# Inverting the 16x16 diagonal blocks of the RWKV-7 chunks row by row on GpSimd instead of by doubling levels on VectorE

## The chip, the cores and the metric

The kernel runs on one core of one Trainium2 chip. The metric is the device time of one execution in microseconds (us). A core has a matrix engine (TensorE, PE in the profile), three engines for elementwise work (VectorE = DVE, ScalarE = ACT, GpSimd = POOL) and a queue that issues DMAs (SyncE = SP). Each engine takes its instructions strictly in the order in which the program lists them; between engines only semaphores order the work.

## The reference, cut to what matters

One block of a hybrid encoder on 256 tokens of width 2048: a norm, one input projection shared by a Mamba-2 SSD mixer and an RWKV-7 time mixer, one output projection, a SwiGLU feed-forward part and a last norm, all in float32. The change is in the RWKV-7 mixer, whose recurrence is, for each of 32 heads of width 64:

```
def step(S, inp):
    r_t, w_t, k_t, v_t, a_t, b_t = inp
    sa = jnp.einsum('bhvk,bhk->bhv', S, a_t)
    S = S * w_t[:, :, None, :] + sa[..., None] * b_t[:, :, None, :] + v_t[..., None] * k_t[:, :, None, :]
    return S, jnp.einsum('bhvk,bhk->bhv', S, r_t)
```

The kernel evaluates it in four chunks of 64 tokens. Inside a chunk the terms `sa` depend on each other through a strictly lower triangular 64x64 matrix N, so the kernel needs the inverse of (I - N) for each head and chunk. It builds that inverse from the inverses X of the 16x16 diagonal blocks, then joins them to 32x32 and 64x64 with small matmuls on TensorE.

## The kernel before, in words

Every large matmul is written as three float32r matmuls: weights arrive by DMA as `raw` tiles (four buffers, SP queue), ScalarE copies them to `whi` (line 192), VectorE subtracts to get `wlo` (line 193), and TensorE multiplies both parts (lines 277 to 279 with 256 columns, 305 to 307 with 512). There are four buffers each of `whi` and `wlo`.

RWKV-7 heads are processed in eight pairs of 128-channel blocks (four heads, times four chunks = 16 head-chunks, times four diagonal blocks = 64 blocks of 16x16). While TensorE runs the projection for one pair, the mixer work of the two previous pairs is interleaved with it. `Side` is a list of functions with due times; every half tick (12 large matmuls of `gemm_a`, or six of `gemm_b`) it emits what is due. A window for a pair is 12 ticks long for the first windows and 16 or more later, when it also holds an output projection. The tables `AMATS`, `INV` and `CHAIN` at the top hold the due ticks. The tile framework then schedules: the order of each engine's queue is fixed when the program is built, by what it expects to be ready, and need not be the emitted one.

The steps for one pair that matter here, in order of dependence:

- `amat("atb", ...)` (lines 602 to 625): TensorE forms N for all chunks (`ps_a`), VectorE masks it.
- `inv_out`: VectorE picks the 16x16 diagonal blocks into `dg` (line 633), SP writes them to a scratch in DRAM (`sc_n`, line 635) and reads them back with one block per partition (`nb`, 64 partitions, line 637). GpSimd sets `xb` to the identity (lines 640 and 641).
- `inv_level(1, 2, 4, 8)`: VectorE doubles the size of the inverted blocks in `xb`: a copy (line 659), then for 2, 4 and 8 two products each, made of a broadcast multiply into `pd` (line 681) and a reduction into `tt` or `xb` (line 683): 1 + 8 + 8 + 4 = 21 instructions a pair.
- `inv_in`: SP writes `xb` to DRAM (`sc_X`, line 691) and reads it back as `cm` (line 694); VectorE masks `cm` into `X` (line 697) and transposes it to `XT` (line 702).
- `lev16a` to `lev32b`: small matmuls `ps_b` (line 708) with VectorE and ScalarE between them make `XF`.
- The chain of the pair before runs in the same window: for each chunk `step_r` (`ps_r`, line 762, reads the state `sn`), `step_w` (`ps_w`, line 776, then `ws` on VectorE, line 780), `step_s` (`ps_s`, lines 792 and 795, then `sn` on VectorE in two instructions, lines 800 and 801). Then `gnorm`, `gnorm2` and `final`, and the output projection `ps_o` with the adds into `h` (line 318).

Of the kernel before, what the change touches and what calls it, by code (L numbers as in the profile page):

```python
# [13 lines left out]
ALU = mybir.AluOpType  # L14
AX = mybir.AxisListType
# [17 lines left out]

PREP = (1.081, 1.2, 4.2, 5.2, 5.536, 6.756, 8.05, 9.2)
AMATS = (0.132, 1.4, 2.027, 2.231, 2.69, 3.323, 6.493)
INV = (4.9, 6.4, 7.9, 9.4, 9.9, 11.9, 12.9, 13.9, 15.9)
STEPS = (0.667, 2.0, 5.0)
SSD = (0.9, 2.7, 4.842, 6.642, 8.442, 8.924, 10.724, 12.524, 12.657, 16.124)
CHAIN = (0.05, 0.6, 1.4, 2.4, 3.4, 4.0, 4.9, 5.9, 6.5, 7.4, 8.4, 9.0, 9.9, 11.4, 12.9, 13.4)
# [29 lines left out]
def tile_hybrid_block(ctx: ExitStack, tc: tile.TileContext, x, norm1_g, w_in, conv_w, conv_b, dt_bias, A_log, D_skip,  # L69
                      ssd_norm_g, mu, w0, w2, a0, a2, g2, k_k, k_a, r_k, gn_w, gn_b, w_out, norm2_g, w_gate, w_up,  # L70
                      w_down, norm_f_g, out):
    nc = tc.nc
    PS = bass.MemoryType.PSUM
    x = x[0]
    out = out[0]
# [10 lines left out]
    side = Side()  # L86
# [7 lines left out]
    def bc(ap, n):  # L94
        return ap.unsqueeze(ap.ndim).broadcast_to(list(ap.shape) + [n])
# [3 lines left out]
    xv = x.rearrange("(b p) d -> p b d", p=P)  # L99
# [52 lines left out]
    for hh in range(2):  # L152
        for s in range(2):
            m = mask2[hh * 64:(hh + 1) * 64, s]
# [4 lines left out]
    for s in range(2):  # L159
        for hh in range(2):  # L160
            a = hh * 64
# [48 lines left out]
    def finish(i, b):  # L210
        r = rstd[i][:, b:b + 1]
        nc.vector.tensor_reduce(r, ssq[i][:, b], axis=AX.X, op=ALU.add)
        nc.scalar.activation(r, r, AF.Sqrt, bias=eps6, scale=1.0 / D)
        nc.vector.reciprocal(r, r)
        return r
# [228 lines left out]
    def rwkv_pair(pi, st):  # L444
        cb0 = 2 * pi

        def tl(name, shape=(P, 2, T), bufs=1, tag=None):
            return rp.tile(list(shape), F32, name=name, tag=tag or name, bufs=bufs)
# [141 lines left out]
        def amat(name, key, half):  # L590
            def f():
                if half == 0:
                    st[name] = tl(name, (P, NCH, 2, 64), 2)
                dst = st[name]
                src = ch(st[key])
                if name == "atb" and half == 1:
                    across(dst, src)
                    return
                ps = mxt("ps_a").rearrange("p (c t) -> p c t", c=4)
                for c in range(4):  # L600
                    for hh in range(2):
                        nc.tensor.matmul(hd(ps, hh)[:, c], hd(src, hh)[:, half * 4 + c],
                                         hd(st["ar"], hh)[:, half * 4 + c].rearrange("p a t -> p (a t)"),
                                         start=True, stop=True)
                nc.vector.tensor_tensor(dst[:, half * 4:half * 4 + 4].rearrange("p c a t -> p c (a t)"), ps,
                                        mask2.rearrange("p a t -> p (a t)").unsqueeze(1).broadcast_to([P, 4, P]),
                                        ALU.mult)
                if name == "atb":
                    d = dst[:, 0:4, 0]
                    nc.vector.tensor_tensor(d, d, bc(st["nn"][:, 0:4], 64), ALU.mult)  # L610
            return f
# [16 lines left out]
        def inv_out():  # L628
            tm = tl("t1", (P, NCH, 4, 16), 2)
            nc.vector.tensor_tensor(tm, st["atb"][:, :, 0].rearrange("p c (b t) -> p c b t", t=16),  # L630
                                    bc(bmask, 16).unsqueeze(1).broadcast_to([P, NCH, 4, 16]), ALU.mult)
            dg = tl("dg", (P, NCH, 16))
            nc.vector.tensor_reduce(dg, tm.rearrange("p c b t -> p c t b"), axis=AX.X, op=ALU.add)
            sc = dram.tile([NCH, P, 16], F32, name="sc_n")
            nc.sync.dma_start(out=sc.rearrange("c p t -> p c t"), in_=dg)
            nb = tl("nb", (64, 272))
            nc.sync.dma_start(out=nb[:, :256].rearrange("p (i t) -> p i t", t=16),
                              in_=sc.rearrange("c (x i) t -> (c x) i t", i=16))
            xb = tl("xb", (64, 272))
            nc.gpsimd.memset(xb, 0.0)  # L640
            nc.gpsimd.memset(xb[:, 0:256:17], 1.0)
            st["nb"], st["xb"] = nb, xb

        def inv_level(s):
            def f():
                nb, xb = st["nb"], st["xb"]
                nm = 8 // s

                def blocks(t, at, swap):

                    v = t[:, :nm * 34 * s].rearrange("p (m x) -> p m x", m=nm)[:, :, at:at + 16 * s]
                    v = v.rearrange("p m (j t) -> p m j t", t=16)[:, :, :, 0:s]
                    return v.rearrange("p m j t -> p m t j") if swap else v


                n21 = blocks(nb, s, False)
                x11 = blocks(xb, 0, True)
                if s == 1:
                    nc.vector.tensor_copy(blocks(xb, 16, False), n21)
                    return  # L660
                x22 = blocks(xb, 17 * s, False)
                x21 = blocks(xb, 16 * s, False)
                tt = tl("tt", (64, 64), 2)

                if s == 2:
                    cut = [(slice(0, nm), r) for r in range(s)]
                    shp = [64, nm, s, s]
                    tv = tt[:, :nm * s * s].rearrange("p (r m c) -> p m r c", r=s, c=s)
                else:
                    cut = [(m, slice(0, s)) for m in range(nm)]  # L670
                    shp = [64, s, s, s]
                    tv = tt[:, :nm * s * s].rearrange("p (m r c) -> p m r c", r=s, c=s)
                tj = tv.rearrange("p m j c -> p m c j")

                def product(out, a, b):

                    for m, r in cut:
                        pd = tl("pd", (64, 512), 2, tag="t1")
                        pv = pd[:, :shp[1] * s * s].rearrange("p (a c j) -> p a c j", c=s, j=s)
                        bb = b[:, m] if s == 2 else b[:, m].unsqueeze(1)  # L680
                        nc.vector.tensor_tensor(pv, a[:, m, r].unsqueeze(2).broadcast_to(shp), bb.broadcast_to(shp),
                                                ALU.mult)
                        nc.vector.tensor_reduce(out[:, m, r], pv, axis=AX.X, op=ALU.add)

                product(tv, n21.rearrange("p m j r -> p m r j"), x11)
                product(x21, x22, tj)
            return f

        def inv_in():
# [160 lines left out]
        def final():  # L850
# [3 lines left out]
            for j in range(2):  # L854
                for kk in range(2):
# [8 lines left out]
            nc.vector.tensor_tensor(yl, yo, yh.bitcast(F32), ALU.subtract)  # L864

        amats = [recept, sums, amat("atb", "bt", 0), amat("atb", "bt", 1), inv_out, amat("atk", "kt", 0),
                 amat("atk", "kt", 1)]
        inv = [inv_level(1), inv_level(2), inv_level(4), inv_level(8), inv_in, lev16a, lev16b, lev32a, lev32b]
        chain = [load2]
        for c in range(4):  # L870
            chain += [step_r(c), step_w(c), step_s(c)]
# [6 lines left out]
    def window(pi, ticks):  # L878
        if pi < 8:
            w = pairs[pi]  # L880
            w["load"]()
            for t, n in zip(PREP, ("decay", "rate", "keys", "keys2", "keysum", "btt", "vt", "ktt")):
                side.at(t, w[n])
        if 0 < pi < 9:
            w = pairs[pi - 1]
            for t, f in zip(AMATS, w["amats"]):
                side.at(t, f)
            for t, f in zip(INV, w["inv"]):
                side.at(t if ticks >= 16 else t * (ticks - 0.5) / 16, f)
        if pi > 1:  # L890
            for t, f in zip(CHAIN, pairs[pi - 2]["chain"]):
                side.at(t if ticks >= 16 else t * (ticks - 0.5) / 16, f)
# [5 lines left out]
    for pi in range(8):  # L898
        st = {}
        pairs.append(rwkv_pair(pi, st))  # L900
        window(pi, 16 if pi > 2 else 12)
        for i, (n, c) in enumerate((("k", CK), ("v", CV), ("r", CR))):
            ps = scaled(gemm_a(w_in, [(0, 256, c + pi * 256)], "ps_rkv"))
            t = pp.tile([P, 2, T], F32, name="rkv", tag="t" + n, bufs=1)
            for j in range(2):
                m = ((c - CR) // P) + 2 * pi + j
                shift(t[:, j], ps[:, j], omA[:, m:m + 1], colA[:, MU + m:MU + m + 1])
            st[n] = t
        out_rwkv(pi - 3)
        side.drain()  # L910


    window(8, 20)
    xzst = ExitStack()

# [6 lines left out]
    for i in range(4):  # L922
# [6 lines left out]
        for j in range(2):  # L929
            b = 2 * i + j  # L930
            conv(BC[:, b // 4, b % 4], ps[:, j], 16 + b)
    nc.scalar.activation(BC, BC, AF.Silu)
    out_rwkv(5)
    side.drain()
    window(9, 18)

    def ssd_group(g, xc, zs):
# [105 lines left out]
    for g in range(4):  # L1043
        xc = []
        for i in range(2):
            ps = scaled(gemm_a(w_in, [(0, 256, CXBC + g * 512 + i * 256)], "ps_xs"))
            t = xz.tile([P, 2, T], F32, name="xc", tag=f"xc{i}")
# [55 lines left out]
    for j in range(D_FF // 512):  # L1103
        c = j * 512
# [28 lines left out]
    for b in range(2):  # L1133
        s = slice(b * P, (b + 1) * P)
        for n, (hi, lo) in enumerate(ws):
# [5 lines left out]
            c = slice(n * 512, (n + 1) * 512)  # L1141
# [6 lines left out]
    for b in range(2):  # L1148
        r = finish(2, b)
        for n in (2, 3, 0, 1):  # L1150
            c = slice(n * 512, (n + 1) * 512)
            t = hg[b][n]
# [33 lines left out]
```

## Time and profile before

| what | value |
|---|---|
| median of three runs | 1677.11 us (1675.01 to 1679.0) |
| the profiled execution: its time / its span | 1676.59 us / 1674.5 us |
| mean granted TensorE clock | 0.996 |
| busy share PE, DVE, ACT, POOL | 98%, 72%, 54%, 1% |
| instructions on POOL | 57 |

The RWKV-7 stage fills about the first 600 us of the span, the SSD stage and its projections follow up to about 960 us, the feed-forward part is the rest. Busy time of PE overlaps: a 256-column matmul is listed with some 0.28 us but the next one starts 0.12 us later, so PE is only idle in the profile where no matmul at all is under way. "Idle before, releaser" tells what an engine waited for.

### The profile page before, as it was taken

Reading aid. Unit: us, or ns where it says so; the run is one execution under the profiler, and the core shown is the slowest. Engines: PE = TensorE matmul, PEld = TensorE weight load, DVE = VectorE, ACT = ScalarE, POOL = GpSimd, SP = SyncE. Lnnn points to the kernel's source line nnn. Section 1 sums busy time; section 2 is a strip of 40 time slices with the busy share of each in tenths; the row PEclk is TensorE's granted clock in tenths of the full one; section 3 lists DMA queues with packets and bytes.
Section 4 is the critical chain, followed back from the end, with each engine's and each line's share of the span. In section 5 each row is a group of like instructions: output and inputs, shape, how many; then the busy total and the mean of one; then the engine's idle time right before and its main releaser. Section 6 shows DMA issues by size and latency. Waiting matters only on the chain.

```text
span 1674.5 us, 31150 instructions
## 1 busy us (share of the span) xinstructions
PE 1641.6 (98%) x12514; PEld 1423.4 (85%) x12514; DVE 1199.3 (72%) x1907; ACT 910.5 (54%) x1488; POOL 17.7 (1%) x57
## 2 busy tenths in 40 slices
PE   8999999999999999999999999999999999999997
PEld 8988888898898998998988888888888888888886
DVE  7888889888898877978778655465465564554657
ACT  6655765757656556667565544444444444444444
POOL 3000000000000000000000000000000000000000
PEclk9999999999999999999999999999999999999999
DMA  9644545445455456675654666666666666666663
GB/s 248 180 127 111 145 125 149 133 133 146 113 151 145 133 173 181 200 217 157 178 173 154 201 190 189 196 191 189 189 190 195 186 196 190 189 189 196 191 190 126
DMA packets 218577, 286.96 MB, mean 171 GB/s; under 512 B 40867, under 2 KB 123585, under 8 KB 217793
## 3 DMA queue, kind: packets, MB, share of 16 engines
q1 hardware_dynamic: 217104, 282.68, 57.9%
q8 instruction: 98, 1.61, 0.4%
q0 software_dynamic: 752, 1.24, 0.3%
q10 hardware_dynamic: 576, 1.05, 0.2%
q14 instruction: 47, 0.38, 0.1%
HBM read 281.75 MB, written 3.18 MB: 170 GB/s over the span
## 4 chain that ended last, share of the span: by engine, by line
PE 79%; DVE 11%; ACT 6%; DMA 2%; issue 2%; SPq 0%; DVEq 0%; ACTq 0%
PE ps_o L305 7%; PE ps_o L307 7%; PE ps_o L306 7%; PE ps_gt L306 5%; PE ps_gt L305 5%; PE ps_up L307 5%; PE ps_gt L307 5%; PE ps_up L305 5%; PE ps_up L306 5%; PE ps_rkv L277 3%; DVE wlo L193 3%; PE ps_rkv L279 2%; PE ps_rkv L278 2%; PE ps_xs L277 2%; PE ps_xs L279 2%; PE ps_xs L278 2%
## 5 line engine op out<-in xcount | busy, mean ns | idle before, releaser
L193 DVE TENSOR_TENSOR wlo<-raw,whi 128x1024 fp32r<-128x1024 f32 x508 | 619.8, 1222 | 368.8 <-ACT whi L192 367.7
L192 ACT CAST whi<-raw 128x1024 fp32r<-128x1024 f32 x508 | 532.3, 1050 | 581.4 <-PE ps_o L307 154.4
L277 PE MATMUL ps_rkv<-uh,whi 128*128 128x256 f32 x768 | 228.3, 297 | 0.0
L279 PE MATMUL ps_rkv<-uh,wlo 128*128 128x256 f32 x768 | 219.6, 286 | 2.5 <-DVE wlo L193 2.5
L278 PE MATMUL ps_rkv<-ul,whi 128*128 128x256 f32 x768 | 219.5, 286 | 0.0
L277 PEld LDWEIGHTS ps_rkv<-uh,whi 128*128 128x128 f32 x768 | 147.5, 192 | 5.9 <-issue 0.5
L279 PEld LDWEIGHTS ps_rkv<-uh,wlo 128*128 128x128 f32 x768 | 147.8, 193 | 3.4 <-DVE wlo L193 2.9
L278 PEld LDWEIGHTS ps_rkv<-ul,whi 128*128 128x128 f32 x768 | 148.2, 193 | 1.1 <-issue 0.3
L305 PE MATMUL ps_gt<-whi,uh 128*128 128x512 f32 x352 | 137.1, 390 | 0.0
L307 PE MATMUL ps_gt<-whi,ul 128*128 128x512 f32 x352 | 137.0, 389 | 0.0
L306 PE MATMUL ps_gt<-wlo,uh 128*128 128x512 f32 x352 | 136.9, 389 | 0.0
L307 PE MATMUL ps_up<-whi,ul 128*128 128x512 f32 x352 | 136.9, 389 | 0.0
L305 PE MATMUL ps_up<-whi,uh 128*128 128x512 f32 x352 | 136.9, 389 | 0.0
L306 PE MATMUL ps_up<-wlo,uh 128*128 128x512 f32 x352 | 136.9, 389 | 0.0
L305 PE MATMUL ps_o<-whi,ah 128*128 128x512 f32 x336 | 131.7, 392 | 0.0
L307 PE MATMUL ps_o<-whi,al 128*128 128x512 f32 x336 | 130.9, 390 | 0.0
L306 PE MATMUL ps_o<-wlo,ah 128*128 128x512 f32 x336 | 130.7, 389 | 0.0
L318 DVE TENSOR_TENSOR h<-ps_o,h 128x512 f32<-128x512 f32 x184 | 120.3, 682 | 6.5 <-PE ps_o L307 6.1
L305 PE MATMUL ps_o<-whi,yh 128*128 128x512 f32 x256 | 106.3, 415 | 3.0 <-DVE h L318 3.0
L306 PE MATMUL ps_o<-wlo,yh 128*128 128x512 f32 x256 | 100.7, 393 | 0.0
L307 PE MATMUL ps_o<-whi,yl 128*128 128x512 f32 x256 | 100.5, 393 | 0.0
L306 PEld LDWEIGHTS ps_up<-wlo,uh 128*128 128x128 f32 x352 | 66.1, 188 | 13.7
(342 smaller groups left out, 2992.4 us busy)
## 6 DMA issues: line engine op xcount, KB each, us to landing
raw<-in_w_in_dram SPq DMA_DIRECT2D x180, 512.0 KB, 4.1
raw<-in_w_gate_dram SPq DMA_DIRECT2D x88, 512.0 KB, 3.7
raw<-in_w_up_dram SPq DMA_DIRECT2D x88, 512.0 KB, 3.7
raw<-in_w_down_dram SPq DMA_DIRECT2D x88, 512.0 KB, 4.6
raw<-in_w_out_dram SPq DMA_DIRECT2D x32, 512.0 KB, 4.3
raw<-in_w_out_dram SPq DMA_DIRECT2D x32, 256.0 KB, 3.4
raw<-in_w_out_dram SPq DMA_DIRECT2D x64, 128.0 KB, 3.3
csb<-cs_d SPq DMA_DIRECT2D x4, 1024.0 KB, 8.0
```

Source lines behind the costliest of these rows:

```text
L192: order(nc.scalar.copy(hi, raw))
L193: order(nc.vector.tensor_tensor(lo, raw, hi.bitcast(F32), ALU.subtract))
L277: nc.tensor.matmul(o, wh, uh[:, kt], start=first and b == 0, stop=False)
L278: nc.tensor.matmul(o, wh, ul[:, kt], start=False, stop=False)
L279: nc.tensor.matmul(o, wl, uh[:, kt], start=False, stop=last and b == 1)
L305: nc.tensor.matmul(ps[b], ah[:, s], hi[:, k], start=first, stop=False)
L306: nc.tensor.matmul(ps[b], ah[:, s], lo[:, k], start=False, stop=False)
L307: nc.tensor.matmul(ps[b], al[:, s], hi[:, k], start=False, stop=last)
L318: nc.vector.tensor_tensor(d, ps[b], d, ALU.add)
```

## The change

VectorE's `inv_level` steps are gone. In their place `inv_rows(0, 15)` emits for each pair a forward substitution on GpSimd, one row of the block after the other: for row i it multiplies the column of N below row i with the finished row i of X (`pd`) and adds the product to all rows below. That is one copy, 14 multiplies and 14 adds, each waiting for the one before (the add of row i writes the row that the multiply of row i+1 reads). `pd` has buffers of its own instead of sharing `t1`. `nb` and `xb` lose 16 unused columns. `INV` gets six entries, and the 12-tick windows get a table `INV12` of their own instead of a scaled one: `inv_in` at 8.4 instead of 7.1, the four level steps at 10.0, 10.5, 11.0, 11.5 instead of 8.6, 9.3, 10.0, 11.4. In the 16-tick windows `inv_in` and the levels keep their ticks (9.9, 11.9, 12.9, 13.9, 15.9).

```
-INV = (4.9, 6.4, 7.9, 9.4, 9.9, 11.9, 12.9, 13.9, 15.9)
+INV = (3.9, 9.9, 11.9, 12.9, 13.9, 15.9)
+INV12 = (3.9, 8.4, 10.0, 10.5, 11.0, 11.5)
...
-        def inv_level(s):
...
+        def inv_rows(i0, i1):
             def f():
...
+                nv = st["nb"][:, :256].rearrange("p (i t) -> p i t", t=16)
+                xv = st["xb"][:, :256].rearrange("p (t c) -> p t c", c=16)
+                for i in range(i0, i1):
+                    n, m = 15 - i, i + 1
+                    below = xv[:, m:, 0:m]
+                    if i == 0:
+                        nc.gpsimd.tensor_copy(below, nv[:, 0, 1:].unsqueeze(2))
+                        continue
+                    shp = [64, n, m]
+                    pd = tl("pd", (64, 64), 2)[:, :n * m].rearrange("p (t c) -> p t c", c=m)
+                    nc.gpsimd.tensor_tensor(pd, bc(nv[:, i, m:], m), xv[:, i, 0:m].unsqueeze(1).broadcast_to(shp),
+                                            ALU.mult)
+                    nc.gpsimd.tensor_tensor(below, below, pd, ALU.add)
             return f
...
-        inv = [inv_level(1), inv_level(2), inv_level(4), inv_level(8), inv_in, lev16a, lev16b, lev32a, lev32b]
+        inv = [inv_rows(0, 15), inv_in, lev16a, lev16b, lev32a, lev32b]
...
-            for t, f in zip(INV, w["inv"]):
-                side.at(t if ticks >= 16 else t * (ticks - 0.5) / 16, f)
+            for t, f in zip(INV if ticks >= 16 else INV12, w["inv"]):
+                side.at(t, f)
```

The built order of the other engines moves with it, although the due ticks of the 16-tick windows are the same. VectorE, a 16-tick window (the fourth pair; the third to the seventh read alike), from the second mask of `atk` to the new state `sn` of the chain, before:

```order
L605 TENSOR_TENSOR atk_3977<-ps_a_4180,mask2_130 128x512
L780 TENSOR_SCALAR ws_4196<-ps_w_4190,nn_2806 128x64
L780 TENSOR_SCALAR ws_4196<-ps_w_4191,nn_2806 128x64
L681 TENSOR_TENSOR pd_4384<-nb_3954,xb_3956 64x512
L193 TENSOR_TENSOR wlo_4429<-raw_4426,whi_4428 128x1024
L575 STREAM_TRANSPOSE btt_4211<-bt_4114 128x512
L800 TENSOR_TENSOR sn_4246<-ps_s_4237,sn_4076 128x128
L575 STREAM_TRANSPOSE ktt_4375<-kt_4116 128x512
L801 TENSOR_TENSOR sn_4246<-sn_4246,pt_1867 128x128
```

The same place after the change (lines are numbered one higher there down to the removed function, and lower behind it):

```order
L606 TENSOR_TENSOR atk_4004<-ps_a_4236,mask2_130 128x512
L755 TENSOR_SCALAR ws_4252<-ps_w_4246,nn_2824 128x64
L755 TENSOR_SCALAR ws_4252<-ps_w_4247,nn_2824 128x64
L672 TENSOR_TENSOR X_4442<-cm_4440,pmask_147 128x256
L677 STREAM_TRANSPOSE XT_4443<-X_4442 128x256
L194 TENSOR_TENSOR wlo_4465<-raw_4462,whi_4464 128x1024
L576 STREAM_TRANSPOSE btt_4267<-bt_4183 128x512
L775 TENSOR_TENSOR sn_4302<-ps_s_4293,sn_4145 128x128
L576 STREAM_TRANSPOSE ktt_4418<-kt_4185 128x512
L776 TENSOR_TENSOR sn_4302<-sn_4302,pt_1876 128x128
```

`X`, which needs the inverse to have gone through DRAM, stood 16 instructions behind that `sn`, next to `mv`; now it stands two places in front of the first `wlo` and ahead of `sn`.

The SP queue in the same window, from the last loads ahead of `sc_X`, before:

```order
L293 DMA raw_4686<-in_w_out_dram 128x512
L295 DMA raw_4686<-in_w_out_dram 64x512 x2
L293 DMA raw_4710<-in_w_out_dram 128x512
L295 DMA raw_4710<-in_w_out_dram 64x512 x2
L691 DMA sc_X_4402<-xb_3956 64x256
L264 DMA raw_4756<-in_w_in_dram 128x4x256
L694 DMA cm_4404<-sc_X_4402 128x8x16
```

And after, from the read-back of `nb`:

```order
L638 DMA nb_3981<-sc_n_3979 64x256
L265 DMA raw_4492<-in_w_in_dram 128x4x256
L666 DMA sc_X_4438<-xb_3983 64x256
L294 DMA raw_4588<-in_w_out_dram 128x512
L296 DMA raw_4588<-in_w_out_dram 64x512 x2
L669 DMA cm_4440<-sc_X_4438 128x8x16
L294 DMA raw_4658<-in_w_out_dram 128x512
```

`sc_X` moved from behind all four weight tiles of the output projection to the front of them, one load behind `nb`; those tiles now queue behind a DMA that waits for GpSimd.

More of the change, by code (lines that the diff above doesn't have):

```diff
@@ L635, in inv_out @@
             nc.sync.dma_start(out=sc.rearrange("c p t -> p c t"), in_=dg)
-            nb = tl("nb", (64, 272))
+            nb = tl("nb", (64, 256))
             nc.sync.dma_start(out=nb[:, :256].rearrange("p (i t) -> p i t", t=16),
                               in_=sc.rearrange("c (x i) t -> (c x) i t", i=16))
-            xb = tl("xb", (64, 272))
+            xb = tl("xb", (64, 256))
             nc.gpsimd.memset(xb, 0.0)
@@ L642, in inv_out @@
             st["nb"], st["xb"] = nb, xb
-        def inv_level(s):
+        def inv_rows(i0, i1):
             def f():
[L646 to L686, printed above, removed]
```

## The prediction

> **What bounds the kernel now.** I read the page first, then the busy times by stretch, then what TensorE waited for in the stage that the change touches.
>
> ```profile
> PE 1641.6 (98%) x12514; PEld 1423.4 (85%) x12514; DVE 1199.3 (72%) x1907; ACT 910.5 (54%) x1488; POOL 17.7 (1%) x57
> ```
>
> ```profile
> 350.00:400.00 50.00, 47.90 (x590) 42.08 (x590) 45.07 (x86) 36.64 (x85) 0.56 (x3) 1.00 0.47 126
> 405.00:440.00 35.00, 35.00 (x441) 33.13 (x438) 29.84 (x63) 16.40 (x43) 0.45 (x2) 1.00 0.47 129
> ```
>
> ```profile
> PE ps_o L305 <- DVE h L318: 3.0, 5, 0.9
> PE ps_b L708 <- DVE X L697: 3.0, 5, 1.3
> PE ps_sum L557 <- ACT kp L516: 3.0, 4, 0.9
> ...
> PE ps_y L810 <- DVE atb L622: 0.5, 1, 0.5
> ```
>
> The columns of the stretches are TensorE, its weight loads, VectorE, ScalarE, GpSimd, then the granted clock (full). TensorE has work all the time in 405 to 440 us, where one pair's inverse is made, and is idle 2.1 us in 350 to 400. Its ten kinds of waits from 95 to 575 us (largest three and last shown) add up to 17.7 us for eight pairs. So TensorE bounds the stage although VectorE is 85 to 90% busy, and taking work off VectorE can win 17.7 us at the very most, about 1%. Any new wait of TensorE costs in full.
>
> **What is removed.** Groups by line, then the copy, all on VectorE:
>
> ```profile
> L681 DVE TENSOR_TENSOR pd<-xb,tt 64x16 f32<-64x16 f32 (+2 forms) x40 | 14.6, 391 | 0.0
> L681 DVE TENSOR_TENSOR pd<-nb,xb 64x16 f32<-64x16 f32 (+2 forms) x40 | 13.5, 365 | 0.6
> L683 DVE TENSOR_REDUCE tt<-pd 64x8 f32<-64x16 f32 (+2 forms) x40 | 10.0, 278 | 0.0
> L683 DVE TENSOR_REDUCE xb<-pd 64x8 f32<-64x16 f32 (+2 forms) x40 | 10.0, 276 | 0.0
> L659 DVE COPY xb<-nb x8: 153/164/168, 101.6 to 549.3; 64x8 f32<-64x8 f32 x8
> ```
>
> That is 48.1 + 1.3 = 49.4 us, 6.2 us a pair. Of TensorE's waits, two kinds stand behind VectorE's backlog and a late X: `ps_o` behind the adds into h, and `ps_b` behind X, 6.0 us over the five pairs with an output projection. I take both as gone: 1.2 us a pair. The `ps_sum` waits end with ScalarE and stay. The smaller tiles and the own buffers of `pd` cost and win nothing: no row waits for them.
>
> **What is added: 29 instructions in a chain on GpSimd.** No multiply or add on GpSimd stands in the trace. The nearest rows of its timeline:
>
> ```profile
> 12.92 1.38 POOL L155 TENSOR_SCALAR_AFFINE_SELECT mask<-mask 64x64 f32<-64x64 f32 x4
> 115.37 0.32 POOL L640 MEMSET xb<- 64x272 f32 x1 [32.82 <-DMA sc_X<-xb]
> 115.75 0.12 POOL L641 MEMSET xb<- 64x16 f32 x1
> ```
>
> Low end: the memset of 16 elements, 0.12 us, plus the 0.06 us between the end of one memset (115.69) and the start of the next: 29 x 0.18 = 5.2 us. The affine select reads, computes and writes 64 partitions of 64 elements in 1.38 / 4 = 0.345 us: 29 x 0.345 = 10.0 us. High end: twice that, 20 us, if a second input stream doubles the time. The new instructions have 15 to 64 elements, 46 in the mean, and two inputs; smaller but with one read more than the select, so I take 10.0 us for the chain, called C from here. [...]
>
> GpSimd is idle otherwise, and behind the 29 instructions stand only memsets for the next pair, due 25 us later. C by itself costs nothing. What counts is who waits for its end.
>
> **What is moved: X ahead of the chain's state on VectorE, and sc_X ahead of the weights on SP.** Take the pair whose `nb` is read back at 409.72. SP's rows, here and of the pair before, and two lines on landing times (of `nb`, then of `cm`):
>
> ```profile
> 366.28 0.47 SPq L691 DMA_DIRECT2D sc_X<-xb  x1
> ...
> 368.26 0.38 SPq L694 DMA_DIRECT2D cm<-sc_X  x1
> ...
> 409.72 0.46 SPq L637 DMA_DIRECT2D nb<-sc_n  x1
> ...
> 417.36 0.35 SPq L293 DMA_DIRECT2D raw<-in_w_out_dram  x1
> ```
>
> ```profile
> DMA to landing us min/median/max: 2.0/3.5/4.3
> ```
>
> ```profile
> DMA to landing us min/median/max: 2.3/3.4/4.0
> ```
>
> VectorE's timeline:
>
> ```profile
> 371.76 0.43 DVE L697 TENSOR_TENSOR X<-cm,pmask 128x256 f32<-128x256 f32 x1 [2.01 <-DMA cm<-sc_X]
> 372.22 0.45 DVE L702 STREAM_TRANSPOSE XT<-X 128x256 f32<-128x256 f32 x1
> ...
> 413.50 0.15 DVE L659 COPY xb<-nb 64x8 f32<-64x8 f32 x1
> ...
> 415.15 0.68 DVE L517 TENSOR_TENSOR kp<-kp,rkv 128x512 f32<-128x512 f32 x1
> ...
> 422.75 0.67 DVE L526 TENSOR_TENSOR kt<-kp,pin 128x512 f32<-128x512 f32 x1
> ...
> 423.96 0.45 DVE L780 TENSOR_SCALAR ws<-ps_w,nn 128x64 f32<-128x64 f32 x2
> ...
> 425.29 1.21 DVE L193 TENSOR_TENSOR wlo<-raw,whi 128x1024 fp32r<-128x1024 f32 x1
> ...
> 427.84 0.24 DVE L801 TENSOR_TENSOR sn<-sn,pt 128x128 f32<-128x128 f32 x1
> ```
>
> TensorE's timeline:
>
> ```profile
> 421.09 0.37 PE L776 MATMUL ps_w<-rs,XF 64*64 64x64 f32 x5
> ...
> 428.65 0.30 PE L762 MATMUL ps_r<-sn,ar 64*64 64x64 f32 x8
> ...
> 442.69 0.50 PE L305 MATMUL ps_o<-whi,yh 128*128 128x512 f32 x1
> ```
>
> When X can start: `nb` lands at 409.72 + 3.5 = 413.2, GpSimd ends at 413.2 + C. `sc_X` to the issue of `cm` took 2.0 us (366.28 to 368.26), `cm` to X 3.5 us (368.26 to 371.76). So X starts at 418.7 + C, with C = 10 at 428.7.
>
> When VectorE gets to X: it now stands right behind `ws`, which needs `ps_w`, ended at 421.46; with the removed work out of the way VectorE is there at about 422. It then waits 428.7 - 422 = 6.7 us with everything behind it: XT, a `wlo`, `btt`, and `sn`.
>
> Who waits for that: `ps_r` on TensorE needs `sn` and came at 428.65; before, `sn` was ready at 428.08, so there is half a us of slack. From X to the end of `sn` stand X and XT (0.43 + 0.45) and the stretch from `wlo` to `sn` (425.29 to 428.08, 2.8 us): 3.7 us. X must start by 428.65 - 3.7 = 425.0, so C may be 6.3 us. At C = 10 TensorE waits 3.7 us. The `wlo` of two later weight tiles are done ahead, so the big matmuls don't run dry first; the small one in front of them holds the queue.
>
> The `sc_X` on SP: the loads of the output projection that stood at 417.36 now leave when GpSimd ends, 423.2 at C = 10, 6 us late. Their first use is at 442.69, so with 3.4 us to land and some 4 us for the issues, the copy and the `wlo` they are in time until GpSimd ends at 435, C = 22. Cost nothing at C = 10, by the 25 us that the load runs ahead.
>
> I count this wait and the gain above for all six pairs in windows of 16 ticks or more, whose VectorE order has X in the same place: 6 x (3.7 - 1.2) = 15 us.
>
> The first two pairs stand in 12-tick windows:
>
> ```profile
> 101.62 0.17 DVE L659 COPY xb<-nb 64x8 f32<-64x8 f32 x1 [0.22 <-DMA nb<-sc_n]
> ```
>
> ```profile
> 120.22 1.27 PE L708 MATMUL ps_b<-X,atb 32*32 32x32 f32 x64
> ```
>
> X can start at 101.6 + 10 + 5.5 = 117.1, and the first `ps_b` now stands 25 large matmuls earlier, 25 x 0.12 = 3 us, at 117.2: nearly in time. But the levels follow at half ticks. VectorE has `ar`, XT, a shift, a `wlo` and two transposes between X and the mask of level 16 (0.7 + 0.45 + 0.5 + 1.2 + 1.4 = 4.2 us), TensorE only 1.3 us of `ps_b` and 11 matmuls of 0.12 us. It waits some 2 us; I take 2 us for each of the two pairs, with zero and 4 as ends: 4 us.
>
> **Sum:** 15 + 4 = +19 us on the profiled execution's 1676.6 (median of the runs 1677.1): 1696 us. The bound for the chances is 0.2% (3.4 us), about what a measurement of this kernel can tell from no change.
>
> **Rivals.**
>
> *GpSimd is quick.* At C below 6.3 us X is in time, TensorE's new wait is gone and the 1.2 us a pair stay won: -7.2 us, less up to 4 us in the first windows: 1671. For it: the memset pitch gives 5.2 us. Against it: a memset reads nothing. At C of 6.5 to 7.5 both cancel: 1676 to 1680, no change.
>
> *GpSimd and VectorE hold each other up.* From 413.5 to 423.4 VectorE runs seven instructions with two inputs in SBUF, the first `kp` and the last `kt` above, with two `wlo`: 5.4 us together. If GpSimd stands still meanwhile, C is 15.4, TensorE waits 9.1 us a pair, the sum is 6 x 7.9 + 2 x 7.4 = +62 us: 1739. Nothing in this trace runs GpSimd's reads beside VectorE, so no row speaks against it. [...]
>
> *VectorE's relief counts for more.* If TensorE's waits behind `wlo` and `ws` go too, up to 8 us more are won (17.7 less the 6.0 counted and the 3.0 of `ps_sum` is 8.7). Alone that doesn't turn the forecast's +19; it widens the low end.
>
> **Chances.** The forecast 0.43; mutual holding 0.25; quick GpSimd 0.18; the cancelling between 0.14. Slower 0.68, within 0.2% 0.14, faster 0.18. Range: 1668, the quick case with a little of the further relief, to 1735, just short of the full holding; some 0.15 is left outside, most of it above. The slower cases alone lie in 1681 to 1740.
>
> **What would show it.** GpSimd rows of `pd` and `xb` with a pitch near 0.35 us, 29 a pair in 10 us (0.2 us: the quick case; gaps as long as VectorE's `wlo`: the holding). VectorE idle 5 to 7 us in front of X, released by the DMA of `cm`, where it was 2 us. TensorE idle 3 to 4 us in front of `ps_r` behind `sn`, once a pair, where it had none. SP waiting for GpSimd at `sc_X`. VectorE's busy time down by 49 us with the span longer. I am wrong if X comes by 425 in the window shown, or if the stall at `ps_r` is given back within the window by waits that I have not counted.

## The result, and the profile after

The changed kernel takes 1736.1 us (median of four runs, 1734.5 to 1739.1) against 1676.2 us for the kernel before, timed beside it: ratio 1.0357, interval 1.0336 to 1.0378. It is 60 us slower. The forecast was 1696 us, with 1668 to 1735 as its range: the direction is right, but the time lies 1 us above the range and the change is three times the +19 us. It is the size of the rival in which GpSimd and VectorE hold each other up (1739 us).

Busy time on the page of after, whose span is 1735.5 us:

```profile
PE 1653.8 (95%) x12514; PEld 1434.1 (83%) x12514; DVE 1161.7 (67%) x1739; ACT 911.0 (52%) x1488; POOL 107.3 (6%) x289
```

VectorE is 38 us less busy than before (1199.3), GpSimd 90 us more. TensorE has the same 12514 instructions and is 12.2 us longer busy with them (1641.6 before). What TensorE waited for from 60 to 660 us, the largest kinds of after, in us in total, times, longest:

```profile
PE ps_r L737 <- DVE sn L776: 39.6, 5, 8.7
PE ps_b L683 <- DVE X L672: 7.6, 1, 7.6
PE ps_y L785 <- DVE ws L755: 5.7, 1, 5.7
PE ps_sum L558 <- ACT kp L517: 3.1, 4, 0.9
PE ps_r L737 <- DVE sn L775: 2.8, 1, 2.8
```

All kinds add up to 65.8 us, 48 us more than the 17.9 before in the same stretch. Forty-eight of waiting and twelve of longer busy time are the 60 us. The first row is the wait that the prediction put at `ps_r`; in five of the six pairs it is 7.3 to 8.7 us long, not 3.7, and in the last pair 2.8.

One pair, step by step (the one whose `nb` is read back at 448.54). SP's rows of after, then GpSimd's, then VectorE's, each with start, duration and the idle time in front:

```profile
448.54 0.46 SPq L638 DMA_DIRECT2D nb<-sc_n  x1
...
465.41 0.48 SPq L666 DMA_DIRECT2D sc_X<-xb  x1
...
467.73 0.59 SPq L669 DMA_DIRECT2D cm<-sc_X  x1
```

```profile
451.63 0.38 POOL L655 COPY xb<-nb 64x15 f32<-64x15 f32 x1 [18.83 <-DMA nb<-sc_n]
...
454.06 0.66 POOL L659 TENSOR_TENSOR pd<-nb,xb 64x55 f32<-64x55 f32 x1
454.80 1.36 POOL L661 TENSOR_TENSOR xb<-xb,pd 64x55 f32<-64x55 f32 x1
456.24 0.62 POOL L659 TENSOR_TENSOR pd<-nb,xb 64x60 f32<-64x60 f32 x1
...
457.31 0.75 POOL L659 TENSOR_TENSOR pd<-nb,xb 64x63 f32<-64x63 f32 x1
...
458.52 1.26 POOL L659 TENSOR_TENSOR pd<-nb,xb 64x64 f32<-64x64 f32 x1
...
460.25 0.74 POOL L659 TENSOR_TENSOR pd<-nb,xb 64x63 f32<-64x63 f32 x1
...
465.17 0.21 POOL L661 TENSOR_TENSOR xb<-xb,pd 64x15 f32<-64x15 f32 x1
```

```profile
453.90 0.68 DVE L518 TENSOR_TENSOR kp<-kp,rkv 128x512 f32<-128x512 f32 x1
...
454.79 1.21 DVE L194 TENSOR_TENSOR wlo<-raw,whi 128x1024 fp32r<-128x1024 f32 x1
455.93 0.78 DVE L523 SCALAR_TENSOR_TENSOR ta<-ta,q 128x512 f32<-128x512 f32 x1
...
457.26 0.64 DVE L525 TENSOR_TENSOR bt<-ta,pin 128x512 f32<-128x512 f32 x1
...
458.42 1.21 DVE L194 TENSOR_TENSOR wlo<-raw,whi 128x1024 fp32r<-128x1024 f32 x1
...
460.18 0.66 DVE L527 TENSOR_TENSOR kt<-kp,pin 128x512 f32<-128x512 f32 x1
...
461.36 0.47 DVE L755 TENSOR_SCALAR ws<-ps_w,nn 128x64 f32<-128x64 f32 x2
471.21 0.43 DVE L672 TENSOR_TENSOR X<-cm,pmask 128x256 f32<-128x256 f32 x1 [9.39 <-DMA cm<-sc_X]
...
474.56 0.25 DVE L776 TENSOR_TENSOR sn<-sn,pt 128x128 f32<-128x128 f32 x1
```

Read GpSimd and VectorE side by side. An operation of GpSimd takes 0.21 to 0.31 us, but six of the 28 take 0.62 to 1.36 us, and each of the six stands over an instruction of VectorE with two inputs in SBUF: `kp`, `wlo`, `ta`, `bt`, `wlo`, `kt`. It ends about 0.15 us behind the end of that instruction. (A seventh, the short `sn` at 454.50, lies between `kp` and the first `wlo`.) Against operations of the same size undisturbed the six lose 3.6 us. The other pairs read alike: of the 224 multiplies and adds of all eight, 42 take over 0.15 us more than the others of their size, and all 42 overlap such an instruction. Once VectorE stands still in front of X (from 461.8), GpSimd starts an operation every 0.28 to 0.37 us to the end. The chain, C, is 13.75 us here, and 12.2 to 13.75 in the eight pairs. TensorE's `ps_r` then comes at 474.86, after 7.28 us of idle time. The clock, by stretch (columns as in the prediction; the last but two is the granted clock):

```profile
467.50:474.80 7.30, 0.08 (x8) 0.00 (x0) 3.55 (x8) 0.90 (x3) 0.39 (x2) 0.78 0.63 164
474.80:478.50 3.70, 3.64 (x28) 3.24 (x28) 2.24 (x4) 2.56 (x7) 0.00 (x0) 0.50 0.36 105
478.50:482.00 3.50, 3.50 (x56) 3.32 (x48) 2.59 (x5) 1.76 (x3) 0.00 (x0) 1.00 0.51 150
```

After the wait TensorE works for 3.6 us at half its clock. Behind the eight long waits of after it does so for 3.2 to 5.8 us, 35 us in all; before has 7 us of it in the same stage. Half of the 28 us between them is 14, which is about the 12 us of longer busy time.

### The profile page after: what moved, and what is told of

Read it like the earlier page. It is cut to its first block, busy times and chain, and to the rows that moved or that the text cites. A ratio compares the mean times of both kernels' runs of the same rounds, so it can differ in the third digit from the quotient of the medians.

```text
span 1735.5 us, 31194 instructions
## 1 busy us (share of the span) xinstructions
PE 1653.8 (95%) x12514; PEld 1434.1 (83%) x12514; DVE 1161.7 (67%) x1739; ACT 911.0 (52%) x1488; POOL 107.3 (6%) x289
## 4 chain that ended last, share of the span: by engine, by line
PE 71%; DVE 9%; ACT 6%; POOL 5%; DMA 5%; issue 2%; SPq 1%; DVEq 0%; ACTq 0%
PE ps_o L306 7%; PE ps_o L308 7%; PE ps_o L307 7%; PE ps_gt L307 5%; PE ps_gt L306 5%; PE ps_up L307 5%; PE ps_gt L308 5%; PE ps_up L308 5%; PE ps_up L306 5%; POOL xb L661 3%; POOL pd L659 3%; DVE wlo L194 3%; PE ps_xs L278 2%; PE ps_rkv L278 2%; PE ps_xs L280 2%
## 5 line engine op out<-in xcount | busy, mean ns | idle before, releaser
L278 PE MATMUL ps_rkv<-uh,whi 128*128 128x256 f32 x768 | 233.0, 303 | 0.0
L278 PEld LDWEIGHTS ps_rkv<-uh,whi 128*128 128x128 f32 x768 | 151.1, 197 | 6.7 <-issue 0.5
L279 PEld LDWEIGHTS ps_rkv<-ul,whi 128*128 128x128 f32 x768 | 151.8, 198 | 0.7 <-issue 0.2
L280 PEld LDWEIGHTS ps_rkv<-uh,wlo 128*128 128x128 f32 x768 | 151.4, 197 | 0.4
L306 PEld LDWEIGHTS ps_up<-whi,uh 128*128 128x128 f32 x352 | 66.1, 188 | 13.7
```

The source lines that it names most:

```text
L278: nc.tensor.matmul(o, wh, uh[:, kt], start=first and b == 0, stop=False)
L279: nc.tensor.matmul(o, wh, ul[:, kt], start=False, stop=False)
L280: nc.tensor.matmul(o, wl, uh[:, kt], start=False, stop=last and b == 1)
L306: nc.tensor.matmul(ps[b], ah[:, s], hi[:, k], start=first, stop=False)
```

## The experiments

Three theories stood at the start. Theory 1: X, which needs GpSimd's chain and two DMAs, stands ahead of `sn` in VectorE's queue, and everything behind it is late. Theory 2: GpSimd's reads beside VectorE cost the time themselves, whatever stands behind X. Theory 3: SP holds the weight loads behind `sc_X`. Every ratio is to runs of the kernel before on the same chip (1675.0 to 1675.6 us; beside after it took 1676.2, so a difference to after is good to about 1 us).

### GpSimd's chain beside the kernel before

```
+    st["xb2"] = tl("xb2", (64, 256))            # set to the identity as xb is
+    side.at(3.9, w["twin"])                     # inv_rows(0, 15) on xb2, pd2
-    cm, tt, red: two buffers
+    cm, tt, red: one buffer
```

> The kernel before, which still inverts by doubling on VectorE, with the same 29 GpSimd instructions a pair added on a tile of their own that nobody waits for; the orders of VectorE, TensorE and SP are those of before. Theory 1: VectorE's two-input instructions grow by some tenths of a us beside GpSimd, nothing waits for GpSimd: 1676 to 1686 us, with GpSimd's chain over 13 us long, as after, since VectorE is busier here. Theory 2 (the contention itself costs the time): 1715 to 1736. Theory 3 has nothing late on SP here: 1676.

1679.2 us, ratio 1.0019 (1.0009 to 1.0028): 3.6 us more. The chain takes 16.0 to 16.4 us in the middle pairs, longer than in after, because VectorE does not stand still beside it. VectorE's busy time grows from 1199.3 to 1202.5 us. So the overlap costs VectorE 3 us at most and the kernel about as much (the single buffers of `cm`, `tt` and `red` are in it too); the rest of theory 2 falls.

### A longer chain

```
 nc.gpsimd.tensor_tensor(below, below, pd, ALU.add)
+if i == 14:
+    for _ in range(6):
+        nc.gpsimd.tensor_tensor(pd, bc(nv[:, i, m:], m), xv[:, i, 0:m]..., ALU.mult)
+        nc.gpsimd.tensor_tensor(below, below, xv[:, 0:1, 1:1 + m], ALU.add)
```

> The kernel after with 12 more GpSimd instructions at the end of each pair's chain (six times the last multiply again, and six adds of zeros to the last row), some 0.28 us apart by the last rows of the chain: C grows by 3.4 us, from 13.6 to 17. VectorE's, TensorE's and ScalarE's orders are those of after. They run while VectorE stands still in front of X. Theory 1: every us of C beyond the first six is a us of TensorE's wait in each of the eight pairs: 8 x 3.4 = 27 us, 1758 to 1768 us. Theory 2 (it is the overlap of GpSimd's reads with VectorE's work that costs): nothing more overlaps, 1736 to 1740 us.

1750.6 us, 14.5 us more than after. The dose was smaller than meant: an added operation does not read what the one just ahead of it wrote, and they follow every 0.17 us, where the chained ones of the same size follow every 0.29 us, so C grew by 2.1 us (15.2 to 16.1 in the first seven pairs). Eight times 2.1 is 17 us. These operations run while VectorE stands still, so nothing more overlaps, and theory 2 expected 0 to 4. A microsecond of C costs about a microsecond in each pair: 0.85 measured.

### X one step later, behind `sn`

```
-nc.vector.tensor_tensor(st["X"]..., ALU.mult)
+tc.keep_in_program_order(nc.vector.tensor_tensor(st["X"]..., ALU.mult))
```

> The kernel after, with X held at its place in the program: on VectorE it comes right behind the new state sn of the chain instead of ahead of it; TensorE's order and GpSimd's work are unchanged. Theory 1 (X, waiting for GpSimd and two DMAs, holds sn and so TensorE): the wait of ps_r for sn (39.6 us in five long waits after) goes; X still waits, now with ws behind it, which ps_y needs, so TensorE loses some 2.7 us a pair in place of 8: 1705 to 1712 us. Theory 2 (it is the contention of GpSimd's reads with VectorE itself that costs, whatever stands behind X): 1736 as after. Theory 3 (late weight loads behind sc_X on SP): also 1736, since SP's order around sc_X hardly changes.

1718.4 us, ratio 1.0252 (1.0237 to 1.0268): 18 us come back, 6 fewer than the least that was expected. The timelines of VectorE, ScalarE and TensorE show what took the place:

```profile
457.32 0.43 DVE L672 TENSOR_TENSOR X<-cm,pmask 128x256 f32<-128x256 f32 x1 [6.44 <-DMA cm<-sc_X]
```

```profile
458.85 0.47 ACT L361 ACTIVATE rkv<-ps_rkv,omA 128x256 f32<-128x256 f32 x1 [5.95 <-DVE ps_rkv L232]
459.23 0.32 ACT L742 COPY rs<-ps_r 128x64 f32<-128x64 f32 x2
```

```profile
459.48 0.60 PE L752 MATMUL ps_w<-rs,XF 64*64 64x64 f32 x8 [4.93 <-ACT rs L742]
```

The wait for `sn` is gone, as theory 1 said. But behind X now stands VectorE's scaling of `ps_rkv`; ScalarE waits for that, and behind it on ScalarE stands the copy `rs`, which the chain's `ps_w` needs. The hold went through two queues instead of one. The expectation had followed VectorE's queue alone.

### X behind the last `ws`

```
+marks["ws"] = nc.vector.tensor_scalar(ws[:, j], ...)
...
+with tc.issue_after(marks["ws"].ins):
     nc.vector.tensor_tensor(st["X"]..., ALU.mult)
```

> The kernel after, with X on VectorE behind the last ws of the chain, some 30 instructions behind dg in the 16-tick windows; GpSimd does the same 29 instructions, TensorE's order is unchanged. Theory 1: X is ready when VectorE gets there, no wait of TensorE stands behind it in those windows, and only the first pairs' loss (some 4 to 10 us) and a longer C remain beside the 6 us of waits won: 1669 to 1685 us. Theory 2 (contention): 1736, GpSimd's chain being as long. Theory 3 (SP's hold at sc_X): 1736.

1706.3 us, ratio 1.0173 (1.0158 to 1.0189): half of the 60 us come back with GpSimd doing all it did. That X's place costs tens of microseconds is shown; the expected 1669 to 1685 is missed, and X still waits for `cm`, 8.7 to 10.2 us in the first two pairs and 0.9 to 3.1 in the next five. From `dg` to `dg` the first two pairs take 5.5 and 9.8 us longer than before, the next five 2.1 to 3.8 each.

### Half of the chain

```
-inv = [inv_rows(0, 15), inv_in, ...
+inv = [inv_rows(0, 8), inv_in, ...
```

> The kernel after with rows 0 to 7 of the substitution alone (rows 8 to 14, which finish the lower rows of each block's inverse, are left out): 15 instructions on GpSimd in place of 29. Theory 1: C falls from 13.6 to some 7 us, so X starts 6 to 7 us earlier, the wait of VectorE before X falls from 9 to 2 to 3 us, and with it TensorE's wait for sn to under 1.5 us a pair: 1676 to 1688 us. Theory 2 (contention, in proportion to the instructions that meet VectorE): half of the loss, about 1705. Theory 3: SP's hold is shorter by the same 6 us and the loss goes too, so this run does not tell it from theory 1.

1707.0 us, ratio 1.0186 (1.0167 to 1.0205). C is 8.3 us in most pairs, and VectorE's wait for `cm` fell from 76.7 to 40.4 us over the eight pairs. Taken alone the time fits theory 2 better than theory 1. But a shorter chain also made the scheduler place X four instructions earlier on VectorE, in front of two `ws`, and TensorE's largest wait is there:

```profile
PE ps_s L770 <- DVE ws L755: 21.5, 6, 4.2
```

The order moved with the dose, so this run does not measure the dose.

### The first two pairs by doubling, as before

```
-inv = [inv_rows(0, 15), inv_in, ...
+inv = ([inv_level(1), ..., inv_level(8)] if pi < 2 else [inv_rows(0, 15)]) + [inv_in, ...
```

> The kernel after, but the two pairs in the 12-tick windows are inverted as before: by doubling on VectorE, with the old due ticks; the six later pairs stay on GpSimd. From dg to dg the first two pairs of after take 5.1 and 6.1 us longer than before. If all of that is X being late in these windows: 1736 - 11 = 1725 us (1721 to 1729). If the prediction's 2 us a pair were the right size there and the rest of the 11 us belongs to what follows: 1732 us.

1725.3 us, ratio 1.0289 (1.0270 to 1.0308): 10.9 us less than after, as the lengths of the two pairs said. The 12-tick windows cost 5.5 us a pair, not the 2 us of the prediction.

### `sc_X` and `cm` off SP

```
-nc.sync.dma_start(out=sc..., in_=st["xb"]...);  nc.sync.dma_start(out=cm, ...)
+nc.gpsimd.dma_start(out=sc..., in_=st["xb"]...);  nc.gpsimd.dma_start(out=cm, ...)
```

> The kernel with X behind the last ws (1706.3 us), with sc_X and cm issued by GpSimd instead of SP, so that the weight loads of the output projection do not queue behind a DMA that waits for GpSimd; the orders of TensorE, VectorE and ScalarE are the same to the instruction. In that kernel the pairs in 16-tick windows still take 2.1 to 3.8 us longer than before (14 us for five), with w_out loads that leave 10 us later than before. Theory 3, for this rest (the held weight loads bunch the copies on ScalarE and make t1s and h late): the rest goes, 1690 to 1697 us. If the hold costs nothing, as the prediction had it: 1706 us.

1698.6 us, 7.7 us less than the same kernel with these DMAs on SP. That is just short of the 1690 to 1697 expected by theory 3, which is right for that much: the prediction's "costs nothing" is wrong once X itself is no longer the last to come.

Both edits together:

> Both together: X behind the last ws, sc_X and cm issued by GpSimd, and the first two pairs by doubling on VectorE as before. If the losses add up: the 15 us of the first two pairs go from the kernel without this edit, 1676 to 1682 us if theory 3 holds for the rest, 1691 us if it does not. Under 1673 us, faster than before, only if VectorE's relief of 6 us a pair wins the 1.2 us of waits a pair that the prediction gave it.

1683.4 us, ratio 1.0050 (1.0033 to 1.0066). The 15 us of the first pairs go, as expected, and 8 us remain, 1 us more than expected. TensorE's largest wait in this kernel is `ps_o` for `h`, 9.8 us in six. The rows of one pair say why: X, still in front of the two `mv` of the norm, waits 2.5 us and makes `mv` late; ScalarE then makes `ysq` late, and VectorE waits 2.83 us for that in front of the next mask and the adds into `h`.

### The order of before, with the inverse on GpSimd

```
-INV = (3.9, 9.9, 11.9, ...
+INV = (3.9, 11.45, 11.9, ...
-with tc.issue_after(marks["ws"].ins):
+with tc.issue_after(marks["mv"].ins):        # the second mv of gnorm
```

> The inverse on GpSimd in the six pairs of the 16-tick windows, X placed on VectorE where the kernel before has it (behind the two mv of the norm), sc_X and cm issued by GpSimd, the first two pairs doubled on VectorE. TensorE's order is that of before to the instruction, VectorE's is that of before without the 21 inversion instructions of each of those six pairs. X can start at 9 + 13.6 = 22.6 us behind the read-back of nb plus what GpSimd's queue adds, before it started 31. Theory 1 (it was the place of X alone): nothing waits for the inverse, and of the 17.7 us of waits of TensorE up to 6 us go (X late, h late): 1669 to 1677 us. If the remaining 8 us of the kernel with X behind the last ws come from GpSimd's reads beside VectorE or from VectorE's instructions growing: still 1680 to 1684 us.

1670.6 us, ratio 0.9976 (0.9965 to 0.9987), against 1675.0: faster than both kernels. X no longer waits and no wait behind it or behind `h` is left of any size:

```profile
408.50 0.47 POOL L656 COPY xb<-nb 64x15 f32<-64x15 f32 x1 [18.75 <-DMA nb<-sc_n]
...
423.65 0.57 POOL L712 DMA_DIRECT2D sc_X<-xb  x1 [0.29 <-POOL xb L662]
```

```profile
432.64 0.16 DVE L855 TENSOR_SCALAR mv<-mv 128x8 f32<-128x8 f32 x1
432.72 0.42 DVE L719 TENSOR_TENSOR X<-cm,pmask 128x256 f32<-128x256 f32 x1
```

```profile
PE ps_sum L559 <- ACT kp L518: 3.9, 5, 0.9
...
PE ps_o L306 <- DVE h L319: 1.2, 5, 0.3
```

The chain takes 14.9 us from its copy to its last add, longer than in after: GpSimd is held up by VectorE as there. That costs nothing, because nothing waits for the chain. For six of the eight pairs GpSimd does what it does in after, and the kernel is 65 us faster. Some 11 of these are the first two pairs; for the rest this run moves X and the two DMAs together, so it speaks for theories 1 and 3 at once.

### The same with the DMAs on SP

```
-nc.gpsimd.dma_start(out=sc...);  nc.gpsimd.dma_start(out=cm, ...)
+nc.sync.dma_start(out=sc...);  nc.sync.dma_start(out=cm, ...)
```

> The same kernel with sc_X and cm on SP again, ahead of the weight loads of the output projection; all other engines keep their order. The hold on SP cost 7.7 us in six pairs with X behind the last ws (1706.3 against 1698.6). If that is the weight loads' own lateness, it costs about as much here: 5 to 9 us over the kernel with these DMAs on GpSimd. If, as the prediction had it, the loads run far enough ahead when nothing else is late: under 2 us.

1686.3 us, ratio 1.0070 (1.0058 to 1.0082): 15.6 us for two DMAs a pair on another queue, about twice what was expected, with the orders of VectorE and ScalarE the same to the instruction. SP's rows, then ScalarE's and VectorE's:

```profile
417.20 0.37 SPq L265 DMA_DIRECT2D raw<-in_w_in_dram  x1
431.65 0.48 SPq L712 DMA_DIRECT2D sc_X<-xb  x1
432.22 0.54 SPq L294 DMA_DIRECT2D raw<-in_w_out_dram  x1
```

```profile
436.93 1.05 ACT L193 CAST whi<-raw 128x1024 fp32r<-128x1024 f32 x1 [1.85 <-DMA raw<-in_w_out_dram]
441.38 1.05 ACT L193 CAST whi<-raw 128x1024 fp32r<-128x1024 f32 x1 [3.40 <-PE ps_rkv L279]
442.33 0.32 ACT L845 COPY Y<-ps_y 128x64 f32<-128x64 f32 x2
```

```profile
442.68 0.69 DVE L854 TENSOR_REDUCE mv<-Y 128x8 f32<-128x512 f32 x1 [2.85 <-ACT Y L845]
```

SP waits 14 us for GpSimd with the weight loads behind it. The late tile holds ScalarE's `whi` at 436.93. The next `whi` waits 3.40 us more, by its row for a matmul of `ps_rkv`; the copy `Y` stands behind it, and `mv`, X and the adds into `h` stand behind `Y`. From the shift of `rkv` ahead of the two `whi` (434.60) to `Y` ScalarE takes 7.7 us; in the kernel with the DMAs on GpSimd the same stretch takes 4.2 (426.33 to 430.55). TensorE pays 9.7 us in six waits at `ps_o`, and behind five of them it works at half its clock for up to 3.4 us (behind the wait of 1.92 us at 458.98 a matmul of 512 columns starts every 0.43 us for 3.4 us, then every 0.23). TensorE needs those weights only much later; ScalarE's queue needs them at once.

### Matmuls that fill the wait

```
+if c == 3 and 0 < pi < 7:
+    for k in range(50):
+        nc.tensor.matmul(pr[0][:, :256], uh[:, k % 16, :P], uh[:, k % 16], start=True, stop=True)
```

> The kernel after with 50 matmuls of 128x256 (6 us at 0.12 us) that nobody needs, put on TensorE ahead of the ps_r that waits for sn, in the six windows with that wait; they overwrite columns of ps_r that the real matmuls then set anew. VectorE's order is the same but for a ws or two. In after TensorE's busy time is 12 us more than before while its waits grew by 48: if that is the clock, lower for some 3 us after each idle of 7 us, it goes when TensorE is kept busy: 1720 to 1727 us although 300 matmuls are added. If the clock has nothing to do with the idle time: 1736 us. If the wait were not there to be filled, the matmuls would add up to 36 us.

1745.2 us, 9 us more than after, where 9 to 16 fewer were expected: TensorE's waits fall by 26 us (65.8 to 39.5), but its busy time grows by 36 (1653.8 to 1689.5). By stretch, behind one filled wait (471.8 to 478.0 is the filler):

```profile
479.30:481.20 1.90, 1.82 (x20) 1.70 (x20) 0.64 (x2) 1.84 (x4) 0.00 (x0) 1.00 0.69 224
481.20:483.60 2.40, 0.15 (x2) 0.00 (x0) 1.68 (x3) 1.09 (x6) 0.00 (x0) 0.99 0.02 3
483.60:486.90 3.30, 3.24 (x20) 3.12 (x21) 2.62 (x5) 1.07 (x3) 0.00 (x0) 0.50 0.49 158
```

With the wait filled the clock stays at 1.00 behind it, where in after it was 0.50: the idle time is what lowers it. But in this kernel the scheduler put ScalarE's copy `rs` behind a shift of `rkv`, TensorE waits 2.3 us for it a little later, and in this window the half clock comes behind that wait instead. What the half clock costs by itself is therefore not separated; that it follows idle time is shown.

## Why the prediction was wrong in size, by its steps

**The place and the mechanism: right.** VectorE was forecast to reach X 12.3 us behind the read-back of `nb` (13.3 measured); `sc_X` to `cm` 2.0 us (2.3), `cm` to X 3.5 (3.5), X to the end of `sn` 3.7 (3.6). The rule "TensorE waits C less 6.3 us" gives 7.45 us for the measured C of 13.75; the row has 7.28. The last pair does not follow it: C is 12.2 there and the wait 2.8. With GpSimd's work unchanged in six pairs, X's place, the queue of two DMAs and the first two pairs put right give back the 60 us and 4 to 5 more.

**C = 10.0 us: the step that failed.** It left out that VectorE holds GpSimd up; C was 12.2 to 13.75 us. Undisturbed it would have been right, as 13.75 less the 3.6 us of holding is 10.1, but by luck: its 0.345 us was the mean of four affine selects, and before's trace has three of these at 0.23 us and one at 0.73.

```profile
L155 POOL TENSOR_SCALAR_AFFINE_SELECT mask<-mask x4: 230/234/732, 12.9 to 13.6; 64x64 f32<-64x64 f32 x4
```

```profile
11.60 1.22 DVE L193 TENSOR_TENSOR wlo<-raw,whi 128x1024 fp32r<-128x1024 f32 x1
...
13.51 0.68 DVE L207 SCALAR_TENSOR_TENSOR sq_v<-h 128x512 f32<-128x512 f32 x1
```

```profile
12.20 0.76 POOL L148 TENSOR_SCALAR_AFFINE_SELECT trimask<-trimask 128x128 f32<-128x128 f32 x1
```

The long one is the last and ends at 14.30, 0.1 us behind VectorE's `sq_v`, which reads `h` twice. The select of 128x128 at 12.20 takes 0.76 us and ends at 12.96, 0.15 us behind a `wlo`; one of the same shape at 2.17 with no such instruction beside it takes 0.29. So the sentence of the prediction that nothing in this trace runs GpSimd's reads beside VectorE is wrong: two rows of before show the holding, and one of them went into the mean that C was worked out from. Selects that are not held give 29 x 0.23 = 6.7 us, by the prediction's own rule no change at all. What brings the undisturbed chain to 10.1 us, the longer two-input operations and the 0.08 us between operations that wait for each other, no row of before shows. The rival's 15.4 was too high, since it took 5.4 us of VectorE's instructions as lost in full, while the operation that is held has its own part in that time. The holding got 0.25. The six long rows above show it one by one, and instructions of VectorE with one SBUF input lengthen nothing there: beside the transpose at 456.63, the reduction at 457.83 and the `ws` at 461.36 GpSimd's operations take 0.30, 0.30 and 0.28 us, as others of their size do. With C = 13.6 the term of the six pairs is 6 x (7.3 - 1.2) = 37 us where the sum had 15.

**The first two pairs: mis-sized.** 4 us in the sum, 10.9 by the run that undoes them; the waits of 7.6 and 5.7 us at `ps_b` and `ps_y` are theirs. This is C again: with X 3.6 us later the prediction's 2 us a pair become 5.6, 11 for the two.

**The clock: missing from the sum.** I counted a wait of TensorE as its length. Behind each of the eight waits it worked 3.2 to 5.8 us at a granted clock of 0.50; its busy time grew by 12.2 us. Behind waits of 1.70, 2.01 and 2.3 us the granted clock was 0.50 as well (last section). By TensorE's own rows the 60 us are 38 of more waiting in the six pairs (37 by the rule), 10 in the first two, and 12 of longer busy time. Little of the 12 is the first two pairs': the run that doubles them on VectorE has TensorE busy no shorter (1655.0 us).

**SP's hold "costs nothing until C is 22": wrong, but hidden.** It asked when TensorE needs the weights. ScalarE's `whi` and what stands behind it need them far sooner. In after no wait for `whi` or `h` behind it stands out (`ps_o` for `h` is 1.3 us), as X is later still; with X out of the way it costs 7.7 us in one layout and 15.6 in the other.

**The gain of 1.2 us a pair: right in kind, smaller.** The order of before with the work off VectorE wins 4.4 us in six pairs, 0.7 each (2 to 6 us by the interval); that kernel also has `sc_X` and `cm` off SP, and no run tells the two apart. VectorE's relief itself was overstated: 38 us less busy, not 49, because the rows of short instructions overlap by some 0.07 us each and I had added their durations.

## What to carry to other kernels

Before moving work to an idle engine, write down what stands behind its consumer in every in-order queue, the DMA queue and the engines behind the first one included: here the same GpSimd chain went with a loss of 60 us or a gain of 4, depending on where one mask stood on VectorE, which queue issued two small DMAs, and whether the two pairs in short windows used it. Keep the order of the engines fixed when the source of a value moves, since due ticks that stay the same do not keep it. Price GpSimd beside VectorE by VectorE's two-input instructions, not by GpSimd's own speed alone (3.6 us of holding came on top of a chain of 10.1), and price a wait of TensorE by its length plus the slow stretch behind it (3.2 to 5.8 us at a clock of 0.50 behind each of the eight here).

## What the runs showed of the hardware

- In after, 42 of the 224 multiplies and adds on GpSimd start during a VectorE instruction with two SBUF inputs, take over 0.15 us more than others of their size and end 0.10 to 0.18 us behind that instruction: 0.29 us become 1.36 beside a `wlo` (at 454.80). VectorE hardly felt it in the kernel with the chain beside before: its busy time grew by 3 us, from 1199.3 to 1202.5, for eight chains, of which the middle ones took 16.0 to 16.4 us each.
- Small two-input GpSimd operations of 64 partitions take 0.21 us (15 elements) to 0.31 us (64) in after. In its chain, where each reads what the one before wrote, they follow some 0.08 us apart; in the longer chain, where none of the added ones reads what the one just ahead wrote, these follow every 0.17 us, less than the 0.21 us of one.
- TensorE's clock was halved behind waits far shorter than 7 us too: behind 2.3 us in the run with filled waits (0.50 from 483.60 to 486.90), and behind 1.9 us in the kernel with X behind the last `ws`, where 512-column matmuls then follow every 0.43 us instead of 0.23 for 3.4 us:

```profile
408.11 0.73 PE L306 MATMUL ps_o<-whi,yh 128*128 128x512 f32 x1 [1.90 <-DVE h L319]
...
409.48 0.63 PE L306 MATMUL ps_o<-whi,yh 128*128 128x512 f32 x1
409.91 0.63 PE L307 MATMUL ps_o<-wlo,yh 128*128 128x512 f32 x1
```

The kernel before shows it too, in its first windows, which the prediction did not use. TensorE waits 2.01 us for a `wlo`, and from about 0.6 us behind the end of that wait it works for 3.4 us at half its clock; behind a wait of 1.70 us at 160.6 the same:

```profile
116.58 0.39 PE L279 MATMUL ps_rkv<-uh,wlo 128*128 128x256 f32 x1 [2.01 <-DVE wlo L193]
```

```profile
117.50:118.50 1.00, 1.00 (x7) 1.00 (x6) 0.78 (x2) 0.35 (x1) 0.00 (x0) 0.50 0.57 86
```

Its gaps of 1.3 and 1.4 us in the later pairs leave the clock at 1.00. So a slow stretch behind a new wait could have been foreseen from before's own trace. A length of wait that decides it does not come out of these runs: with the DMAs on GpSimd and X behind the last `ws` a wait of 1.92 us at 471.2 leaves the clock at 1.00, and in the kernel with both edits one of 1.36 us at 535.5 is followed by 3.4 us at 0.50. In after the stretches at 0.50 that go with the eight waits last 3.4, 6.8 or 10.2 us, part of which falls into the wait itself.
